# Layer 1's weight and rotation splits moved to GpSimd, in a two-layer attention trunk on one core

## The chip, the cores and the metric

The kernel runs on one core of one Trainium2 chip. The metric is device time in microseconds (us), the median of several executions. The engines are called as the profile calls them: PE (TensorE, the matmuls), PEld (its weight loads), DVE (VectorE), ACT (ScalarE), POOL (GpSimd) and SP (SyncE, which here issues every DMA). All arithmetic is float32. A product of two float32 operands is made from three matmuls: each operand is split into a rounded high part and the remaining low part, and high by high, high by low and low by high are summed.

## The reference, cut to what matters

Two decoder layers work on 1024 tokens of width 1024. Layer 0 mixes with a dilated sliding-window attention in three groups, layer 1 with a differential attention; each is followed by a gate, an output projection and a norm. The change is in layer 1, whose mixer is, shortened:

```
proj = h @ w_in
q = rope(proj[..., :1024]);  k = rope(proj[..., 1024:2048])
v = proj[..., 2048:3072];    gate = proj[..., 3072:]
for each head h of 8 and each block of 128 queries:
    s = q k^T / 8            # two score maps c = 0, 1, causal
    p = softmax(s)
    a = p[0] - lam * p[1]
    o = a @ v
y = (rmsnorm(o) * (1 - lambda_init) * silu(gate)) @ w_out
```

## The kernel before, in words

**Two kinds of order.** PE's instructions run in the order in which the program writes them (manual schedule for PE). The order on DVE, ACT, POOL and SP is set by a scheduler that simulates the program when it is built; each engine then runs its own list in order, and waits where an operand isn't ready.

**Units.** Layer 1's query and key projections are made in eight units, one a head, by `qk_unit` (L220), called with `on_pool=True` from `filler1` (L1022). A unit has two weight halves. Each half is loaded to `raw`, cast by ACT to `wh` (L184, the high part) and subtracted to `wl` (L122 through `split`, the low part). The tags `wh` and `wl` have three buffers, so a half can be split as soon as the half three places earlier has been used up; layer 1's value weights (`values1`, L811) take their turn in the same buffers.

A unit then makes four projections of 24 matmuls of 512 columns: two chunks of 512 tokens, each for both halves, into two PSUM banks (tag `pj`, L274, `pqk` in the trace). ACT copies each bank to an SBUF tile `x` (L243); POOL, which reads no PSUM here, rotates: four products and two sums, L247 to L252, into the tiles `r[0]` and `r[1]`. `x` has two buffers and L252 is the last reader of both, so the next chunk's copies wait for L252, and the matmuls that need the bank again wait for the copy. After the second chunk ACT casts each `r` to `rh` (L256), a subtraction overwrites `r` with its low part (L122 through `low`), and SP stores both to HBM (`qk_d`, L259), from where `heads_in` loads them as `qh`, `ql`, `ka` (L266, L268) when a head is due.

**Interleaving.** `Filler` feeds the units between the steps of the attention. First it runs 2.4 units alone (`LEAD1`), here called the lead; then each head's scores (L921, into two banks of tag `s`), exponentials (L931), transposes (L954), products with the values (L974) and norms alternate with the remaining units, value blocks and gates. DVE empties a score bank with the mask and the row minimum (L924); the matmuls of the score after next wait for that. Other DVE work in line with it: the minima (L927, L930), the combination of the two maps (L940, L941, L943), the low parts `pl` of the transposed weights, and the low parts of `wl` and `r`.

**Who subtracts, before.** `split` without an engine takes `alt()` (L125), which gives DVE and POOL in turn; in layer 1's units this puts the first half on POOL and the second on DVE. Both `r` subtractions of a layer 1 unit are on DVE (L257).

## Time and profile before

| | |
|---|---|
| median of 3 runs | 2029.63 us (2026.72 to 2030.63) |
| the profiled execution's own time | 2031.38 us |
| its span, first to last instruction | 2029.5 us |
| mean granted PE clock | 0.981 |
| layer 1's lead | about 1439 to 1495 us of the span |
| layer 1's interleaved part | about 1495 to 1960 us |

The profiled execution is one run of its own: 1.75 us above the median, with 1.9 us of its time outside the span. A timeline row gives the start, the duration, the engine, the line, the operation and its tiles, and in brackets the idle time of the engine just before it and what ended it. A row of the windows view gives busy time and instruction count of PE, PEld, DVE, ACT and POOL in a stretch, the granted PE clock, the share of busy DMA engines and GB/s.

### The profile page before, as it was taken

The page shows a single profiled execution, that of the slowest core. Times are in us where ns is not written, and L with a number is a line of the kernel's source. Part 1 is how long each engine was busy: PE and PEld are TensorE (multiplying, and loading weights), DVE is VectorE, ACT ScalarE, POOL GpSimd, SP SyncE. Part 2 cuts the span into 40 slices and gives each one's busy share as a digit, 9 for nine tenths or more (in the row PEclk, how much of TensorE's full clock was granted, in tenths as well). Part 3 has the DMA queues.
Part 4 walks back from the last instruction along what each step waited for, and adds up shares of the span by engine and source line. Part 5 has one row for each costly group of instructions (what it writes and reads, how often), then busy time and mean ns, then how long its engine had stood idle before and what let it go on. Part 6 is the DMA issues. An engine that isn't in the chain of part 4 may idle for free.

```text
span 2029.5 us, 28888 instructions
## 1 busy us (share of the span) xinstructions
PE 1905.9 (94%) x10008; PEld 1594.5 (79%) x10008; DVE 1143.0 (56%) x2771; ACT 888.0 (44%) x2057; POOL 618.0 (30%) x386
## 2 busy tenths in 40 slices
PE   6999999999999998989898978899999999999898
PEld 4788888888878787878787867788878788887776
DVE  3312122146676768676768674571057877878626
ACT  3312122125555555555555565352244445545632
POOL 2000000043353535353535340040471533524111
PEclk8999999999999999999999989999999999999999
DMA  5424244377696969697878889553356555555753
GB/s 208 146 88 140 87 156 152 113 221 229 191 300 195 291 202 293 195 282 218 267 234 240 256 284 294 162 176 107 129 174 193 175 176 164 169 196 182 274 160 125
DMA packets 218018, 397.90 MB, mean 196 GB/s; under 512 B 40976, under 2 KB 123408, under 8 KB 217872
## 3 DMA queue, kind: packets, MB, share of 16 engines
q1 hardware_dynamic: 217872, 396.04, 61.3%
q8 instruction: 80, 1.31, 0.3%
q14 instruction: 66, 0.54, 0.1%
HBM read 254.87 MB, written 132.71 MB: 191 GB/s over the span
## 4 chain that ended last, share of the span: by engine, by line
PE 62%; DMA 13%; DVE 12%; ACT 4%; POOL 4%; issue 3%; SPq 1%; POOLq 0%; DVEq 0%; ACTq 0%
PE pqk L274 22%; PE pv L213 16%; PE pg L274 8%; PE po L386 4%; PE sc L921 2%; PE pe L439 2%; PE up L646 2%; PE sc L596 2%; DMA wb<-wt_d 2%; PE ob L974 2%; DMA st_d<-st 2%; PE tp L619 2%; DVE u L669 1%; POOL r L252 1%; DVE pm L924 1%
## 5 line engine op out<-in xcount | busy, mean ns | idle before, releaser
L274 PE MATMUL pqk<-XL,wh 128*128 128x512 f32 x1024 | 421.1, 411 | 0.0
L274 PE MATMUL pqk<-XH,wh 128*128 128x512 f32 x1024 | 409.3, 400 | 1.7 <-DVE t L251 1.7
L274 PE MATMUL pqk<-XH,wl 128*128 128x512 f32 x1024 | 410.5, 401 | 0.0
L606 ACT ACTIVATE pm<-pm,st 128x128 f32<-128x128 f32 (+1 forms) x384 | 170.2, 444 | 159.7 <-DVE st L603 158.1
L122 POOL TENSOR_TENSOR wl<-raw,wh 128x1024 fp32r<-128x1024 f32 x35 | 84.0, 2400 | 500.6 <-ACT wh L184 500.6
L274 PEld LDWEIGHTS pqk<-XH,wh 128*128 128x128 f32 x1024 | 194.3, 190 | 30.6 <-DVE t L251 2.4
L274 PEld LDWEIGHTS pqk<-XL,wh 128*128 128x128 f32 x1024 | 194.4, 190 | 27.5
L274 PEld LDWEIGHTS pqk<-XH,wl 128*128 128x128 f32 x1024 | 194.8, 190 | 27.0
L250 POOL TENSOR_TENSOR r<-t 128x512 f32<-128x512 f32 x64 | 98.2, 1535 | 266.7 <-DVE t L249 265.7
L122 DVE TENSOR_TENSOR wl<-raw,wh 128x1024 fp32r<-128x1024 f32 x61 | 82.0, 1345 | 149.1 <-ACT wh L184 148.6
L213 PE MATMUL pv<-vwh,XH 128*128 128x512 f32 x384 | 155.8, 406 | 7.0 <-ACT XH L158 4.0
L184 ACT CAST wh<-raw 128x1024 fp32r<-128x1024 f32 x96 | 100.5, 1047 | 140.3 <-PE pqk L274 61.8
L213 PE MATMUL pv<-vwl,XH 128*128 128x512 f32 x384 | 154.9, 403 | 2.8 <-POOL vwl L122 2.8
L213 PE MATMUL pv<-vwh,XL 128*128 128x512 f32 x384 | 154.8, 403 | 0.9 <-DVE XL L122 0.3
L122 DVE TENSOR_TENSOR vs<-pv,vs 128x512 fp32r<-128x512 f32 x64 | 44.2, 691 | 197.3 <-ACT vs L513 191.3
L931 ACT ACTIVATE pm<-pm,mx 128x256 f32<-128x256 f32 (+7 forms) x128 | 99.4, 776 | 120.3 <-DVE mx L930 61.8
L122 DVE TENSOR_TENSOR pp<-tp,pp 128x512 fp32r<-128x512 f32 (+2 forms) x192 | 104.0, 542 | 73.6 <-ACT pp L623 72.0
L619 PE MATMUL tp<-ident,pm 128*128 128x128 f32 x560 | 95.7, 279 | 39.2 <-DVE pp L122 38.2
L603 DVE CUSTOM_DVE_ANT_0 pm<-sc,masks 128x128 f32<-128x128 f32 (+1 forms) x384 | 118.8, 344 | 20.8 <-PE sc L596 19.4
L619 PEld LDWEIGHTS tp<-ident,pm 128*128 128x128 f32 x560 | 72.6, 143 | 73.5 <-issue 34.2
L924 DVE CUSTOM_DVE_ANT_0 pm<-sc,md 128x512 f32<-128x512 f32 (+3 forms) x192 | 102.5, 551 | 32.9 <-PE sc L921 30.1
L513 ACT CAST vs<-pv 128x512 fp32r<-128x512 f32 x48 | 28.2, 587 | 189.9 <-PE pv L213 188.7
(514 smaller groups left out, 4483.6 us busy)
## 6 DMA issues: line engine op xcount, KB each, us to landing
qk_d<-rh SPq DMA_DIRECT2D x64, 512.0 KB
qk_d<-r SPq DMA_DIRECT2D x64, 512.0 KB
qh<-qk_d SPq DMA_DIRECT2D x128, 256.0 KB
ql<-qk_d SPq DMA_DIRECT2D x128, 256.0 KB
ka<-qk_d SPq DMA_DIRECT2D x64, 512.0 KB
v_d<-vs SPq DMA_DIRECT2D x48, 512.0 KB
raw<-in_dil_qk_dram SPq DMA_DIRECT2D x48, 512.0 KB
vt<-v_d SPq DMA_DIRECT2D x48, 512.0 KB
```

The costliest lines, as they stand in the source:

```text
L122: eng.tensor_tensor(o, full, hi.bitcast(F32), ALU.subtract)
L184: nc.scalar.copy(wh, raw)
L213: nc.tensor.matmul(o, lhsT=l, rhs=r_, start=first and k == 0, stop=last and k == 3 * KT - 1, skip_group_check=True)
L250: nc.gpsimd.tensor_sub(put(r[0]), nat(t1), nat(t2))
L274: nc.tensor.matmul(o, lhsT=l[:, kt, :], rhs=r_[:, kt, tok], start=kt == 0 and k == 0, stop=kt == KT - 1 and k == 2)
L386: nc.tensor.matmul(banks[c], lhsT=l[:, kt, ts(n)], rhs=r_[:, ts(c, 512)], start=first and k == 0, stop=last and k == 2,)
L439: nc.tensor.matmul(bank, lhsT=l[:, kt, ts(n)], rhs=r_[:, ts(c, 512)], start=kt == 0 and k == 0, stop=kt == EARLY - 1 and k == 2)
L603: nc.vector.tensor_tensor_reduce(pm[:, cols], sc[:, cols], m[:, m.shape[1] - w_ :], 1.0, 3.0e38, ALU.add, ALU.min, st[:, 0, j : j + 1])
L606: nc.scalar.activation(pm[:, cols], pm[:, cols], AF.Exp, bias=st[:, 0, j : j + 1], scale=-1.0, accum_out=st[:, 1, j : j + 1])
L619: nc.tensor.transpose(out=tp[:, ts(n)], in_=self.pb.pop((b, kb)), identity=ident)
L924: nc.vector.tensor_tensor_reduce(pm[:, k0:k1], sc[:, :w_], m_, 1.0, 3.0e38, ALU.add, ALU.min, mx[:, j : j + 1])
L931: nc.scalar.activation(pm[:, :wq], pm[:, :wq], AF.Exp, bias=mx[:, 0:1], scale=-1.0, accum_out=den)
```

## The change

In layer 1's units both weight halves' subtractions, and both `r` subtractions, are given to POOL. Layer 0's calls (`on_pool=False`) still take `alt()`.

```
-            split(wh, wl, load(w[half], [P, KT, P]))
+            split(wh, wl, load(w[half], [P, KT, P]), nc.gpsimd if on_pool else None)
...
-            low(nc.vector if on_pool else alt(), r[e].bitcast(F32R), r[e], rh)
+            low(nc.gpsimd if on_pool else alt(), r[e].bitcast(F32R), r[e], rh)
```

Each unit made two calls of `alt()` in `split`, an even number, so every later user of `alt()` keeps its engine. Eight `wl` and sixteen `r` subtractions of 128x1024 move from DVE to POOL. PE's list is unchanged; the scheduler's lists for DVE, ACT, POOL and SP are the same up to the end of layer 1's gates, and differ in places after that.

POOL, in the lead, from the first unit's second chunk (`x_13168`, `x_13169`) to the second unit's first (`x_13258` is its first product). `wl_13339` is the third unit's first half. Before:

```order
L247 TENSOR_TENSOR t_13172<-x_13168,cos_2235 128x512
L248 TENSOR_TENSOR x_13168<-x_13168,sin_2236 128x512
L122 TENSOR_TENSOR wl_13339<-raw_13340,wh_13338 128x1024
L249 TENSOR_TENSOR t_13173<-x_13169,sin_2236 128x512
L250 TENSOR_TENSOR r_13054<-t_13172,t_13173 128x512
L251 TENSOR_TENSOR x_13169<-x_13169,cos_2235 128x512
L252 TENSOR_TENSOR r_13055<-x_13169,x_13168 128x512
L247 TENSOR_TENSOR t_13258<-x_13254,cos_2235 128x512
```

Now, in the same place (`wl_13197` is the second unit's second half):

```order
L122 TENSOR_TENSOR wl_13197<-raw_13198,wh_13196 128x1024
L247 TENSOR_TENSOR t_13172<-x_13168,cos_2235 128x512
L248 TENSOR_TENSOR x_13168<-x_13168,sin_2236 128x512
L122 TENSOR_TENSOR wl_13339<-raw_13340,wh_13338 128x1024
L249 TENSOR_TENSOR t_13173<-x_13169,sin_2236 128x512
L250 TENSOR_TENSOR r_13054<-t_13172,t_13173 128x512
L251 TENSOR_TENSOR x_13169<-x_13169,cos_2235 128x512
L122 TENSOR_TENSOR r_13054<-r_13054,rh_13180 128x1024
L252 TENSOR_TENSOR r_13055<-x_13169,x_13168 128x512
L122 TENSOR_TENSOR r_13055<-r_13055,rh_13185 128x1024
L247 TENSOR_TENSOR t_13258<-x_13254,cos_2235 128x512
```

A `wl` stands ahead of the chunk, one `r` ahead of its L252, and the other `r` ahead of the next unit's first product.

ACT, the end of the second unit (`x_13316` and `x_13317` are the copies of its second chunk) to the first copy of the third (`x_13467`), as a difference. `wh_13344` is the third unit's second half, `wh_13652` the first value weights after it, `pm0` and `pm1` the first exponentials of head 0:

```order
 L184 CAST wh_13344<-raw_13346 128x1024
+L184 CAST wh_13652<-raw_13654 128x1024
 L243 COPY x_13316<-pqk_13266 128x512
-L184 CAST wh_13652<-raw_13654 128x1024
 L243 COPY x_13317<-pqk_13291 128x512
 L256 CAST rh_13328<-r_13202 128x1024
+L931 ACTIVATE pm0_13414,den_13393<-pm0_13414,mx0_13415 128x128
+L931 ACTIVATE pm1_13423,mx1_13424<-pm1_13423,mx1_13424 128x128
 L256 CAST rh_13333<-r_13203 128x1024
 L243 COPY x_13467<-pqk_13352 128x512
```

The cast of the value weights, whose buffer comes free when the second unit's last projection ends, now stands ahead of the copy of that unit's third projection; and two exponentials stand ahead of the second `rh`.

DVE, around the fourth unit's `r` subtractions, at the start of head 2 (`pm_14660` and `pm_14688` are score tiles), as a difference:

```order
 L122 TENSOR_TENSOR pl<-tp,ph 128x512
-L122 TENSOR_TENSOR r<-r,rh 128x1024
 L924 ISA pm_14660,mx_14661<-sc,md 128x128
 L924 ISA mx_14661 128x1
-L122 TENSOR_TENSOR r<-r,rh 128x1024
 L940 RECIPROCAL mx_14661<-mx_14661 128x1
+L941 SCALAR_TENSOR_TENSOR mx_14661<-mx_14661,neg_lam,den 128x1
+L943 SCALAR_TENSOR_TENSOR pm_14641<-pm_14660,mx_14661,pm_14641 128x128
 L924 ISA pm_14688,mx_14689<-sc,md 128x256
```

The two `r` rows go, and L941 and L943 of the map before move up into the room.

## The prediction

> **What bounds the kernel now.** I read the page first, then the windows of layer 1, PE's waits there, and the timelines of the engines around them. The page's first part:

> ```profile
> PE 1905.9 (94%) x10008; PEld 1594.5 (79%) x10008; DVE 1143.0 (56%) x2771; ACT 888.0 (44%) x2057; POOL 618.0 (30%) x386
> ```

> PE is the bound, and DVE or POOL matter only where PE waits for them. The windows view (PE, PEld, DVE, ACT, POOL busy; PE clock; DMA share; GB/s) splits layer 1's attention: two stretches of one unit each in the lead, then the interleaved part.

> ```profile
> 1439.20:1461.70 22.50, 22.50 (x99) 18.23 (x98) 1.23 (x1) 5.74 (x8) 13.28 (x9) 1.00 0.46 155
> 1461.70:1484.20 22.50, 22.50 (x98) 18.02 (x97) 3.68 (x3) 6.34 (x9) 19.07 (x13) 1.00 0.67 206
> 1497.00:1960.00 463.00, 434.70 (x2670) 381.31 (x2670) 342.26 (x940) 239.72 (x468) 164.75 (x112) 0.99 0.56 180
> ```

> In the lead a unit takes PE 22.5 us without a gap, so a projection takes 5.6 us; POOL is busy for 19.07 of the second 22.5 us and DVE for 3.68. In the interleaved part it is the other way about: DVE is 74% busy, POOL 36%. PE's waits from 1440 to 1960 us (total, times, longest):

> ```profile
> PE sc L921 <- DVE mx L924: 18.3, 18, 2.5
> PE sc L921 <- issue: 3.8, 1, 3.8
> PE sc L921 <- DMA ka<-qk_d: 1.1, 1, 1.1
> ```

> What there is to win is mainly the 18.3 us in which a score's matmuls wait until DVE has emptied their bank. PE doesn't wait for POOL anywhere, but in the lead it is a near thing. ACT there:

> ```profile
> 1471.03 1.05 ACT L256 CAST rh<-r 128x1024 fp32r<-128x1024 f32 x1 [2.44 <-POOL r L252]
> 1471.99 0.58 ACT L243 COPY x<-pqk 128x512 f32<-128x512 f32 x1
> 1483.85 1.05 ACT L184 CAST wh<-raw 128x1024 fp32r<-128x1024 f32 x1 [1.46 <-PE pqk L274]
> ```

> and PE, at the projection that reuses the bank which that copy empties:

> ```profile
> 1472.62 0.50 PE L274 MATMUL pqk<-XH,wh 128*128 128x512 f32 x1
> ```

> L252 ends at 1471.0, the cast and the copy follow, the copy ends at 1472.57 and the projection starts at 1472.62. The slack is nil: whatever delays this L252 delays PE.

> **The change part by part.** The groups view of 1440 to 1960 us gives the moved work (count, busy us, mean ns):

> ```profile
> L122 DVE TENSOR_TENSOR wl<-raw,wh 128x1024 fp32r<-128x1024 f32 x16 | 21.6, 1351 | 39.3 <-ACT wh L184 39.1
> L122 DVE TENSOR_TENSOR r<-r,rh 128x1024 fp32r<-128x1024 f32 x16 | 21.2, 1330 | 19.6 <-ACT rh L256 19.6
> L122 POOL TENSOR_TENSOR wl<-raw,wh 128x1024 fp32r<-128x1024 f32 x9 | 21.6, 2401 | 71.3 <-ACT wh L184 71.3
> ```

> DVE loses 8 x 1.35 + 16 x 1.33 = 32.1 us, POOL gains 24 x 2.40 = 57.6 us. Seven of the 24 belong to the lead (three `wl`, four `r`), seventeen to the interleaved part, which has 12 `r` and 5 `wl`.

> *The lead.* A unit would cost POOL 19.07 + 3 x 2.40 = 26.3 us against PE's 22.5, so POOL can't keep up there. The rows that I step through are these of POOL:

> ```profile
> 1462.48 2.40 POOL L122 TENSOR_TENSOR wl<-raw,wh 128x1024 fp32r<-128x1024 f32 x1 [1.82 <-ACT wh L184]
> 1464.84 1.30 POOL L249 TENSOR_TENSOR t<-x,sin 128x512 f32<-128x512 f32 x1
> 1467.46 1.29 POOL L251 TENSOR_TENSOR x<-x,cos 128x512 f32<-128x512 f32 x1
> 1468.84 2.17 POOL L252 TENSOR_TENSOR r<-x 128x512 f32<-128x512 f32 x1
> ```

> The extra `wl` ahead of the first unit's second chunk fits into the idle 1.82 us and the rest before 1462.48, where POOL must wait for ACT's cast anyway, so L251 still ends at 1468.75. Then `r` (2.40) and L252 (1.30, since no DVE work crosses it any more) end at 1472.5 instead of 1471.0. Cast and copy end at 1474.1, and PE waits from 1472.7 to about 1474.1: 1.4 us. The second `r` starts only after its cast, at 1473.6, and ends at 1476.0; the second unit's first chunk, with a `wl` in it, then ends at 1476.0 + 5 x 1.3 + 2.4 + 1.3 = 1486.2. Meanwhile PE finishes that unit at 1485.4 and wants its bank back. On ACT the cast of the value weights now stands ahead of that copy, and its buffer comes free only at PE's end: cast 1.05 and copy 0.58, 1487.0, so PE waits 1.7 us more. After that the attention is mixed in, a unit takes PE longer than POOL, and POOL catches up. Together **+3.1 us**. The bounds: 0 if the scheduler's order leaves the copies earlier than I read it, and 6.5 if each wait also brings 1.7 us of lower clock. Two windows, the first after PE's longest wait for DVE, the second after a shorter one, and that shorter wait:

> ```profile
> 1525.50:1528.90 3.40, 3.40 (x19) 3.40 (x18) 2.49 (x6) 2.15 (x4) 0.00 (x0) 0.50 0.48 189
> 1870.70:1874.10 3.40, 3.40 (x21) 2.88 (x21) 3.38 (x10) 3.33 (x6) 0.00 (x0) 1.00 0.53 151
> ```

> ```profile
> 1867.51 0.51 PE L921 MATMUL sc<-ka,qh 128*128 128x512 f32 x1 [2.08 <-DVE mx L924]
> ```

> Half clock for 3.40 us followed a wait of 2.53 us (its row is below), full clock one of 2.08 us; I take no loss for waits of 1.4 and 1.7. [...]

> *The relief.* Where DVE's own `r` stood ahead of a bank that PE waited for, the wait should go (timeline rows of DVE and PE, in order of time):

> ```profile
> 1493.36 1.23 DVE L122 TENSOR_TENSOR r<-r,rh 128x1024 fp32r<-128x1024 f32 x1 [2.27 <-ACT rh L256]
> 1494.85 0.39 PE L921 MATMUL sc<-ka,qh 128*128 128x256 f32 x1 [0.83 <-DVE mx L924]
> 1608.78 1.22 DVE L122 TENSOR_TENSOR r<-r,rh 128x1024 fp32r<-128x1024 f32 x1
> 1610.46 0.45 PE L921 MATMUL sc<-ka,qh 128*128 128x384 f32 x1 [0.81 <-DVE mx L924]
> 1613.24 0.44 PE L921 MATMUL sc<-ka,qh 128*128 128x384 f32 x1 [1.24 <-DVE mx L924]
> 1667.06 0.33 PE L921 MATMUL sc<-ka,qh 128*128 128x128 f32 x1 [1.13 <-DMA ka<-qk_d]
> 1728.31 0.44 PE L921 MATMUL sc<-ka,qh 128*128 128x384 f32 x1 [1.25 <-DVE mx L924]
> 1733.17 0.50 PE L921 MATMUL sc<-ka,qh 128*128 128x512 f32 x1 [0.31 <-DVE mx L924]
> 1738.69 0.38 PE L921 MATMUL sc<-ka,qh 128*128 128x256 f32 x1 [1.53 <-DVE mx L924]
> ```

> I count 0.83, 0.81, 0.31 and 1.13 whole (the load of `ka` was issued behind a store that waited for DVE after two `r`), and half of 1.24, 1.25 and 1.53, where other DVE work was late as well: **-5.1 us**, between -3.1 and -7.1.

> *The price.* POOL's work holds up DVE. In the timelines, POOL first, then DVE and PE:

> ```profile
> 1515.73 2.40 POOL L122 TENSOR_TENSOR wl<-raw,wh 128x1024 fp32r<-128x1024 f32 x1 [3.91 <-ACT wh L184]
> ```

> ```profile
> 1516.39 1.77 DVE L927 TENSOR_TENSOR mx<-mx 128x1 f32<-128x1 f32 x1
> 1519.51 1.27 DVE L941 SCALAR_TENSOR_TENSOR mx<-mx,neg_lam,den 128x1 f32<-128x1 f32 x1
> 1520.81 1.99 DVE L943 SCALAR_TENSOR_TENSOR pm<-pm,mx,pm 128x768 f32<-128x768 f32 x1
> ```

> ```profile
> 1523.46 0.50 PE L921 MATMUL sc<-ka,qh 128*128 128x512 f32 x1 [2.53 <-DVE mx L924]
> 1563.21 0.38 PE L921 MATMUL sc<-ka,qh 128*128 128x256 f32 x1 [0.72 <-DVE mx L924]
> 1849.39 0.39 PE L921 MATMUL sc<-ka,qh 128*128 128x256 f32 x1 [1.38 <-DVE mx L924]
> ```

> ```profile
> L927 DVE TENSOR_TENSOR mx<-mx x64: 140/155/2252, 1507.2 to 1932.6; 128x1 f32<-128x1 f32 x64
> ```

> A subtraction of one element a partition, 155 ns as a rule, took 1.77 us and ended when POOL's 2.40 us piece did. Seven pieces of 2.40 us already run on POOL in the interleaved part (the group's nine less two in the lead), and three of PE's waits (2.53, 0.72, 1.38) come within a few us after one: 0.66 us a piece at most, and nothing at the least, since in the first of them later POOL work shares the blame. I take 0.3, nearer the two plain cases spread over seven: 17 x 0.3 = **+5.1 us**, between 0 and 11.2.

> [...]

> *At no cost.* The `r` stores to HBM start up to 2.7 us later in the lead; the first score there starts 3 us later too. Later units are stored most of a head before they are loaded. POOL's `r` work delays L1004 (the norm's power) by at most one piece, in front of a gate that is due later. ACT's work is the same in amount.

> The sum is 3.1 - 5.1 + 5.1 = +3.1 us: 2034.5 against the profiled execution's own 2031.38. That execution is 1.75 us above the median, 2029.63; against the median it is **2032.7 us**.

> **The rivals.** A difference under 0.2% (4 us) can hardly be told from none in this kernel.

> *POOL's backlog lasts (slower).* The waits of the lead are read whole or worse: the copy of the third unit's first projection is also late, because two exponentials and a second `r` stand ahead of it (about 2 us), and one wait brings half clock (1.7 us): 3.1 + 2 + 1.7 = 6.8. It decides if PE loses over 5 us before 1500 us. For it: POOL's 26.3 against 22.5 us. Against: 2.4 units only.

> *The lock eats the relief (slower).* Every added piece holds DVE for half its length: 17 x 1.2 = 20.4 us against 17 x 1.34 = 22.8 us taken off in the interleaved part, so DVE wins nothing and the pieces come at moments that the scheduler didn't plan. With 0.66 us a piece and the relief at 3.1: 3.1 - 3.1 + 11.2 = +11.2, or 2040.8. It decides if DVE's mean for L927, L941 and L943 rises. The two together are what "slower" stands for: 2038 in the middle.

> *DVE's relief carries (faster).* The lead's waits are hidden and the added pieces meet DVE in L924 and `pl`: 0 - 7.1 + 1 = -6, 2023.6. For it: 74% busy on DVE, 36% on POOL. Against: the nil slack at 1472.6.

> **How the numbers follow.** The forecast, a change too small to tell: 0.45. The two slower rivals together 0.40, since two separate mechanisms lead there and the sum already leans that way; faster 0.15. The range goes from -4.6 (most of the faster rival) to +10.4 (just short of the lock's full price): 2025 to 2040.

> **What would show it.** Right: POOL's idle time in the lead gone; PE idle for 1 to 2 us near 1473 and near 1486, each ended by ACT's copy; no `r` ahead of the first score; POOL about 58 us and DVE about 12 to 20 us changed in busy time over layer 1; PE's wait for L924 near 18 us still. Wrong: PE without a gap before 1495 us, or its wait for L924 below 10 or above 28 us.

## The result and the profile after

The changed kernel takes 2041.65 us, the median of its five undisturbed runs (2040.24 to 2045.93; a sixth, at 2623.72 us and a granted clock of 0.656 against 0.976 to 0.980 in the five, is left out). The kernel before, run beside it, takes 2032.03 us over six runs. The ratio, worked out over the runs, is 1.0055, with a 95% interval from 1.0035 to 1.0075 (the two medians, 9.6 us apart, give 1.0047): slower by about 0.5%. The forecast was +3.1 us and 2032.7 us, with 2040 as the upper end; both were too low. The profiled execution took 2044.94 us, with a span of 2043.1.

The page's first part, of the kernel after:

```profile
PE 1912.1 (94%) x10008; PEld 1599.8 (78%) x10008; DVE 1136.3 (56%) x2747; ACT 886.1 (43%) x2057; POOL 666.5 (33%) x410
```

POOL has 48.5 us more and DVE only 6.7 us less, though 24 pieces of 1.3 us left DVE and came to POOL at 2.40 us. The windows of the lead and of the interleaved part (PE, PEld, DVE, ACT, POOL busy; PE clock; DMA share; GB/s):

```profile
1461.70:1484.20 22.50, 21.23 (x92) 16.91 (x91) 0.00 (x0) 6.13 (x8) 20.11 (x13) 1.00 0.36 134
...
1497.00:1973.00 476.00, 444.51 (x2708) 388.83 (x2707) 347.93 (x931) 241.78 (x477) 214.83 (x136) 0.99 0.55 181
```

In this stretch of the lead DVE now does nothing at all (0.00 us) while POOL is busy for 20.11 of 22.5 us, and PE has lost its unbroken 22.50. PE's waits from 1440 to 1975 us (total, times, longest):

```profile
PE sc L921 <- DVE mx L924: 18.8, 17, 2.5
PE tp L954 <- DVE pl L122: 4.1, 4, 2.2
PE pqk L274 <- ACT x L243: 2.7, 2, 1.4
...
PE sc L921 <- issue: 2.2, 1, 2.2
...
PE sc L921 <- DMA ka<-qk_d: 1.2, 1, 1.2
```

The wait for L924 is where it was (18.3 before), and the two waits for ACT's copies `x` are new. They are the forecast's two, as PE's rows and ACT's rows ahead of them show (the cast of `rh` ahead of the first copy, the cast of the value weights ahead of the second):

```profile
1480.18 0.50 PE L274 MATMUL pqk<-XH,wh 128*128 128x512 f32 x1 [1.27 <-ACT x L243]
...
1493.07 0.50 PE L274 MATMUL pqk<-XH,wh 128*128 128x512 f32 x1 [1.43 <-ACT x L243]
```

```profile
1478.60 1.05 ACT L256 CAST rh<-r 128x1024 fp32r<-128x1024 f32 x1 [3.81 <-POOL r L252]
1479.55 1.06 ACT L243 COPY x<-pqk 128x512 f32<-128x512 f32 x2
...
1491.49 1.04 ACT L184 CAST wh<-raw 128x1024 fp32r<-128x1024 f32 x1 [4.55 <-PE pqk L274]
1492.44 1.07 ACT L243 COPY x<-pqk 128x512 f32<-128x512 f32 x2
```

**Where the time went.** PE's list is the same in every kernel below, so the start of the same matmul can be compared between two traces. The two profiled executions were already 6.2 us apart at the start of layer 1, in code that is unchanged and runs in the same order on PE, DVE, ACT and POOL; that is chance (the last section says what goes with it) and is taken off. What a kernel adds to the trace of before from there on, worked out from the starts of PE's matmuls at 1400, 1493, 1596 and 1795 us of before and at the end:

| kernel | lead, to 1493 | first heads, to 1596 | to 1795 | to the end | sum |
|---|---|---|---|---|---|
| whole change, first profile | +3.1 | +5.4 | +3.4 | -4.6 | +7.3 |
| whole change, second profile | +3.1 | +7.6 | +5.1 | -4.6 | +11.1 |
| `lead_only` | +3.1 | +3.5 | -0.3 | +0.9 | +7.2 |
| `later_only` | 0.0 | -0.4 | +3.6 | -1.6 | +1.6 |
| `lead_r_dve` | +0.1 | +2.9 | +6.7 | -2.7 | +6.9 |
| `short_rope` | +0.8 | -3.7 | -2.9 | -4.0 | -9.7 |

Single profiles differ by some 3 us, so the sums are a map and the medians decide. The lead's +3.1 is the forecast to a tenth, and then comes as much again that the forecast didn't have.

DVE's operations were held more often. The groups of four operations of DVE that have two inputs in SBUF (count, busy us, mean ns), before and after, over the same 1497 to 1985 us:

```profile
L943 DVE SCALAR_TENSOR_TENSOR pm<-pm,mx,pm 128x128 f32<-128x128 f32 (+3 forms) x64 | 62.7, 980 | 1.2
L941 DVE SCALAR_TENSOR_TENSOR mx<-mx,neg_lam,den 128x1 f32<-128x1 f32 x64 | 22.7, 355 | 1.3
L927 DVE TENSOR_TENSOR mx<-mx 128x1 f32<-128x1 f32 x64 | 22.0, 344 | 0.7
...
L1005 DVE TENSOR_TENSOR nr<-nr,nd 128x4 f32<-128x4 f32 x16 | 4.7, 296 | 12.8 <-POOL nr L1004 12.8
```

```profile
L943 DVE SCALAR_TENSOR_TENSOR pm<-pm,mx,pm 128x128 f32<-128x128 f32 (+3 forms) x64 | 71.9, 1124 | 1.3
...
L927 DVE TENSOR_TENSOR mx<-mx 128x1 f32<-128x1 f32 x64 | 25.0, 391 | 0.8
L941 DVE SCALAR_TENSOR_TENSOR mx<-mx,neg_lam,den 128x1 f32<-128x1 f32 x64 | 24.1, 376 | 1.4
...
L1005 DVE TENSOR_TENSOR nr<-nr,nd 128x4 f32<-128x4 f32 x16 | 9.3, 583 | 12.0 <-POOL nr L1004 12.0
```

Their sum goes from 112.1 to 130.3 us for the same work. "The four groups" below is this sum; it gauges how long POOL holds DVE. Some expectations use a wider gauge, "DVE's excess": what all of DVE's operations of the interleaved part took beyond the time of the same operation undisturbed, 54.5 us before and 74 to 75 in the two profiles after.

### The profile page after: what moved, and what is told of

Same layout as the page of the kernel before. It is cut to its first block, busy times and chain, and to the rows that moved or that the text cites. A ratio compares the mean times of both kernels' runs of the same rounds, so it can differ in the third digit from the quotient of the medians.

```text
span 2043.1 us, 28875 instructions
## 1 busy us (share of the span) xinstructions
PE 1912.1 (94%) x10008; PEld 1599.8 (78%) x10008; DVE 1136.3 (56%) x2747; ACT 886.1 (43%) x2057; POOL 666.5 (33%) x410
## 5 line engine op out<-in xcount | busy, mean ns | idle before, releaser
L274 PE MATMUL pqk<-XL,wh 128*128 128x512 f32 x1024 | 423.5, 414 | 0.0
L274 PE MATMUL pqk<-XH,wh 128*128 128x512 f32 x1024 | 411.0, 401 | 4.3 <-ACT x L243 2.7
L274 PE MATMUL pqk<-XH,wl 128*128 128x512 f32 x1024 | 412.8, 403 | 0.0
L122 POOL TENSOR_TENSOR wl<-raw,wh 128x1024 fp32r<-128x1024 f32 x43 | 104.0, 2418 | 495.8 <-ACT wh L184 495.7
L274 PEld LDWEIGHTS pqk<-XH,wh 128*128 128x128 f32 x1024 | 195.3, 191 | 34.8 <-ACT x L243 3.6
L274 PEld LDWEIGHTS pqk<-XH,wl 128*128 128x128 f32 x1024 | 196.3, 192 | 27.2
L274 PEld LDWEIGHTS pqk<-XL,wh 128*128 128x128 f32 x1024 | 195.7, 191 | 27.6
L122 DVE TENSOR_TENSOR wl<-raw,wh 128x1024 fp32r<-128x1024 f32 x53 | 70.4, 1329 | 168.0 <-ACT wh L184 167.9
L184 ACT CAST wh<-raw 128x1024 fp32r<-128x1024 f32 x96 | 100.5, 1047 | 144.6 <-PE pqk L274 71.1
L122 DVE TENSOR_TENSOR vs<-pv,vs 128x512 fp32r<-128x512 f32 x64 | 44.1, 689 | 196.6 <-ACT vs L513 191.8
L122 DVE TENSOR_TENSOR pp<-tp,pp 128x512 fp32r<-128x512 f32 (+2 forms) x192 | 103.8, 541 | 75.3 <-ACT pp L623 73.7
L924 DVE CUSTOM_DVE_ANT_0 pm<-sc,md 128x512 f32<-128x512 f32 (+2 forms) x192 | 102.9, 550 | 39.1 <-PE sc L921 36.4
```

Of the source, the lines that this page charges most:

```text
L122: eng.tensor_tensor(o, full, hi.bitcast(F32), ALU.subtract)
L184: nc.scalar.copy(wh, raw)
L274: nc.tensor.matmul(o, lhsT=l[:, kt, :], rhs=r_[:, kt, tok], start=kt == 0 and k == 0, stop=kt == KT - 1 and k == 2)
L924: nc.vector.tensor_tensor_reduce(pm[:, k0:k1], sc[:, :w_], m_, 1.0, 3.0e38, ALU.add, ALU.min, mx[:, j : j + 1])
```

## The experiments

Three theories stood against one another. *Lead*: the loss is paid in units 24 to 26 and the first heads. *Lock*, the forecast's word for DVE's operations held while a piece of POOL runs: the pieces hold DVE and eat what it was relieved of. *Order*: the scheduler's order alone. All times are medians with the kernel before run beside them (2032.6 to 2034.5 us); the ratios are worked out over the runs. Code is cut to the lines that differ, from the kernel after in `r_only`, `wl_only`, `lead_r_dve` and `x_dve`, from the kernel before in the others.

| kernel | us | ratio to before | 95% interval | four groups, us |
|---|---|---|---|---|
| `r_only` | 2040.21 | 1.0032 | 1.0016 to 1.0048 | 127.3 |
| `wl_only` | 2035.16 | 0.9998 | 0.9984 to 1.0013 | 115.1 |
| `later_only` | 2034.82 | 1.0000 | 0.9986 to 1.0015 | 126.6 |
| `no_sub` | 2027.06 | 0.9960 | 0.9943 to 0.9977 | 102.3 |
| `lead_only` | 2039.24 | 1.0036 | 1.0023 to 1.0049 | 113.4 |
| `again` | 2042.42 | 1.0046 | 1.0030 to 1.0062 | 131.5 |
| `extra_sub` | 2065.88 | 1.0167 | 1.0149 to 1.0185 | 134.0 |
| `extra_set` | 2033.18 | 1.0004 | 0.9992 to 1.0016 | 107.3 |
| `extra_set5` | 2039.41 | 1.0032 | 1.0018 to 1.0047 | 110.4 |
| `extra_short` | 2050.12 | 1.0086 | 1.0060 to 1.0111 | 126.8 |
| `quarters` | 2040.54 | 1.0034 | 1.0020 to 1.0048 | 115.2 |
| `wl_dve` | 2034.75 | 1.0007 | 0.9993 to 1.0021 | 107.2 |
| `lead_r_dve` | 2036.16 | 1.0017 | 1.0002 to 1.0032 | 132.1 |
| `x_dve` | 2047.34 | 1.0072 | 1.0053 to 1.0092 | 132.4 |
| `short_rope` | 2024.19 | 0.9958 | 0.9943 to 0.9973 | 97.3 |

### Which part costs

**`r_only`**: the change's second line alone.

```
-            split(wh, wl, load(w[half], [P, KT, P]), nc.gpsimd if on_pool else None)
+            split(wh, wl, load(w[half], [P, KT, P]))
```

> Only the sixteen r subtractions of layer 1 go to POOL; the weight halves stay in turn on POOL and DVE. The lock theory (each POOL piece of 2.4 us in the interleaved part holds up DVE, and what DVE is spared is eaten by that): 12 of the 17 pieces of the interleaved part are here, about 0.5 us each, so +6 us, and +1.4 to +3 us in the lead from the r that stands ahead of L252: +7 to +9 us against before, DVE's L927, L941 and L943 together some 14 us longer. The backlog theory (POOL can't keep up in the lead, the rest is even): +3 to +5 us, all of it before the first score. The theory that it is only the scheduler's new order: anything within 5 us of before, unrelated to the count of pieces.

**`wl_only`**: its first line alone.

```
-            low(nc.gpsimd if on_pool else alt(), r[e].bitcast(F32R), r[e], rh)
+            low(nc.vector if on_pool else alt(), r[e].bitcast(F32R), r[e], rh)
```

> Only the second weight halves go to POOL; the r subtractions stay on DVE. Lock: 5 pieces of the interleaved part, +2 to +3 us against before, no wait in the lead. Backlog: under +2 us, POOL's extra 2.4 us a unit fits into the lead. Order: anything within 5 us of before.

**`later_only`**: both lines, `nc.gpsimd` only if `unit >= 27`; as before in units 24 to 26.

> The change for units 3 to 7 alone, so that nothing of it lies in the lead: 15 pieces of 2.4 us, all in the interleaved part. Lock: 15 x 0.5 = +7 to +8 us against before, with no wait of PE for ACT's copies before the first score. Backlog: no change against before, within 2 us. Order: within 5 us of before, either way.

**`no_sub`**: no subtraction in layer 1's units at all; the third matmul of a projection reads `wh` again, and `r` is stored as it is in place of its low part.

```
-        low(eng or alt(), wl, raw, wh)
+        eng == 0 or low(eng or alt(), wl, raw, wh)
...
-            split(wh, wl, load(w[half], [P, KT, P]))
-            tiles.append((wh, wl))
+            split(wh, wl, load(w[half], [P, KT, P]), 0 if on_pool else None)
+            tiles.append((wh, wh if on_pool else wl))
...
-            low(nc.vector if on_pool else alt(), r[e].bitcast(F32R), r[e], rh)
+            on_pool or low(alt(), r[e].bitcast(F32R), r[e], rh)
```

> Layer 1's 32 subtractions of both kinds are left out on every engine (the third matmul takes the high part again, and the full r is stored as its low part), so that neither DVE nor POOL does them. Lock: DVE's relief without a price, and POOL's own eight pieces gone too: -7 to -12 us against before. Backlog: -5 us, the relief that was forecast. Order: no sign can be told, within 5 us of before.

`r_only` has most of the loss, `wl_only` and `later_only` have none that shows (their intervals are 3 us wide to either side). For `later_only` the lock theory had asked for +7 to +8 us; measured is 1.0000, although the four groups rose to 126.6. So from unit 27 on the holds and the relief come to nothing in the sum, and the loss that shows lies in units 24 to 26. All 32 subtractions together are worth 0.4% (`no_sub`), 7.4 us; its interval doesn't tell the lock theory's -7 to -12 from the -5 of the others.

**`lead_only`**: the reverse of `later_only`, `nc.gpsimd` only if `24 <= unit < 27`. **`again`**: the whole change unaltered.

> The splits and the halves r of units 24 to 26 alone go to POOL; from unit 27 on all is as before. The lead theory (what the change costs is paid in the lead and in the first heads, where DVE has nothing else to do and POOL is in the way of ACT's copies of x and of the heads' own loads): +6 to +10 us against before, all of it ahead of 1580 us of the trace, with the two waits of PE for ACT's x (1.28 and 1.43 us in the changed kernel) there again. The lock theory (a piece on POOL holds DVE's operations for 1.2 us, 17 times, in the interleaved part): +2 to +4 us, the two waits alone.

> The whole change once more, as a yardstick for the parts and for a second profile of it. Every theory: +8 to +12 us against before; the waits of PE in layer 1 between 30 and 35 us in its profile, 32.7 us the first time. If it comes out under +5 us, the first result was high by chance, and the prediction's +3 would be near.

The lead theory is borne out: +0.36%, against +0.46 and +0.55% for the whole. The two parts add up within their intervals; the 3 us by which the medians of the whole (+9.5 and +9.6 us) lie above that of `lead_only` (+6.4) are placed by no run. PE's waits of `lead_only` from 1440 to 1600 us:

```profile
PE sc L921 <- DVE mx L924: 5.8, 4, 2.5
PE pqk L274 <- ACT x L243: 2.7, 2, 1.4
PE sc L921 <- DMA ka<-qk_d: 0.8, 1, 0.8
PE tp L954 <- DVE pl L122: 0.5, 1, 0.5
```

The waits for `x` are 2.7 us of the +7.2 in its trace. Comparing matmul by matmul with before gives the next +3.5: PE is 3.1 us behind at 1485 us, 1.9 at 1501, 2.9 at 1506.5, 4.4 at 1510.5, 5.5 at 1548 (the 0.55 us for `pl` is in it) and 6.5 at 1553. Two waits of before, 0.83 and 1.76 us, became one of 2.40, at 1506.78, no loss by itself, but behind it the granted clock was 0.50 for 3.40 us. Held operations had a part in that wait: at 1498.60 and 1499.43 DVE's L941 and L943 took 0.80 and 1.48 us, against 0.22 and 0.48 in before, under POOL's late `r` and the rotation behind it. The windows around the wait:

```profile
1503.60:1507.00 3.40, 1.00 (x5) 0.60 (x4) 3.40 (x5) 0.18 (x1) 3.32 (x3) 1.00 0.01 2
1507.00:1510.40 3.40, 3.40 (x10) 2.73 (x10) 2.86 (x11) 2.30 (x4) 0.45 (x1) 0.50 0.00 0
```

PE is idle for 2.40 of the first 3.40 us, and the second stretch runs at 0.50; over it the matmuls fall 1.5 us further behind. Of the last us, 0.81 is a wait for the second head's keys, at 1553.43. That head's own `r` went out by 1500 us; what is late is the third unit's. Its stores stood ahead of all loads of the second head on SP, and now two of them stand between these loads. SP before, then in `lead_only`:

```profile
1528.01 0.52 SPq L259 DMA_DIRECT2D qk_d<-r  x1
1531.27 1.13 SPq L266 DMA_DIRECT2D qh<-qk_d  x2
...
1538.95 0.58 SPq L268 DMA_DIRECT2D ka<-qk_d  x1
```

```profile
1533.83 0.49 SPq L266 DMA_DIRECT2D qh<-qk_d  x1
1534.42 0.54 SPq L259 DMA_DIRECT2D qk_d<-rh  x1
...
1536.58 0.56 SPq L259 DMA_DIRECT2D qk_d<-r  x1
...
1543.64 0.51 SPq L268 DMA_DIRECT2D ka<-qk_d  x1
```

The last load of the keys goes out 9.8 us after the head's first load, 7.7 before.

**`lead_r_dve`**: the whole change, with the six `r` of the lead back on DVE.

```
-            low(nc.gpsimd if on_pool else alt(), r[e].bitcast(F32R), r[e], rh)
+            low(nc.gpsimd if unit >= 27 else nc.vector if on_pool else alt(), r[e].bitcast(F32R), r[e], rh)
```

> The whole change, except that the halves r of units 24 to 26 stay on DVE, which does nothing in the lead; the weights' splits of all units and the r from unit 27 on are on POOL. If the six r pieces of the lead are what costs (ACT's x waits behind the cast of rh, and the first heads' keys come late): no wait for x, no wait for ka in the second head, and 0 to +3 us against before, so that 6 us and more of the whole change's loss are gone. If the loss sits in all pieces alike (lock theory by count, 6 of 17): two thirds of it stay, +6 to +8 us.

+0.17%: by the two ratios about two thirds of the loss goes with six of the 24 pieces. The upper end of its expectation, +3 us, is just passed (2036.16 against 2032.63). PE's waits from 1440 to 1600 us have one row left, no `x`, no `ka`, and the third unit's stores stand ahead of the second head's loads again:

```profile
PE sc L921 <- DVE mx L924: 8.2, 7, 2.5
```

**`x_dve`**: the whole change, with the lead's copies `x` taken from ACT.

```
-                    nc.scalar.copy(x[i], pp[i])
+                    (nc.vector.tensor_copy if unit < 27 else nc.scalar.copy)(x[i], pp[i])
```

> The whole change, with the copies x of units 24 to 26 made by DVE in place of ACT, so that they don't stand behind the casts of rh on ACT. If the two waits of PE for x (1.28 and 1.43 us) come from ACT's order, they shrink to under 0.5 us each, and what follows from them does too: 2 to 5 us faster than the whole change. If x waits for POOL to let its tile go, the waits stay above 1 us and the time is that of the whole change.

A miss. The first wait went: the copy now starts as soon as POOL's L252 lets its tile go (DVE's first row below). The second grew from 1.43 to 2.90 us, since on DVE the copy stands behind a split of weights that waits for its own cast:

```profile
1474.77 1.29 DVE L243 COPY x<-pqk 128x512 f32<-128x512 f32 x2 [9.86 <-POOL r L252]
1487.88 1.23 DVE L122 TENSOR_TENSOR wl<-raw,wh 128x1024 fp32r<-128x1024 f32 x1 [11.81 <-ACT wh L184]
1489.02 1.28 DVE L243 COPY x<-pqk 128x512 f32<-128x512 f32 x2
```

So ACT's order makes the first wait, and moved to DVE the second copy is late again, behind other work in line. Whether the whole is slower than the change isn't shown, since the intervals overlap; a wait of 4.68 us near 1535 us in its trace stays unexplained.

The order theory wasn't tested by itself. DVE's list of layer 1's attention differs from that of before in every kernel of the table, so an effect of some us from a new order can lie in any of the differences. Against it as the main cause: the two waits for `x` are the same, 1.3 and 1.4 us, in all three traces with the lead's whole pieces on POOL and the copies on ACT, and `lead_r_dve` and `later_only` have none.

### What a piece on POOL costs

**`extra_sub`**, **`extra_set`**, **`extra_set5`**, **`extra_short`**: before, with extra work on POOL behind each half of the weights of units 27 to 31, written to the tile `raw`, which nobody reads any more. Nothing is taken from DVE.

```
-            split(wh, wl, load(w[half], [P, KT, P]))
-            tiles.append((wh, wl))
+            split(wh, wl, raw := load(w[half], [P, KT, P]))
+            [low(nc.gpsimd, raw, raw, wh) for _ in range(2 * (unit >= 27))]; tiles.append((wh, wl))
```

In `extra_set` the call is `nc.gpsimd.memset(raw, 0.0)`, in `extra_set5` five of it, in `extra_short` eight subtractions of two of the eight tiles each.

> Before, with two subtractions 128x1024 more on POOL behind each half of the weights of units 27 to 31 (20 in all; they write to a tile that is no longer read). Nothing is taken from DVE, so this is the price alone. The lock theory: each holds DVE's operations for about 1.2 us, some 20 to 24 us of holds in the sum, and the kernel is 7 to 12 us slower. The lead theory: the holds fall mostly where PE has work in hand, 0 to +4 us.

> The same as extra_sub, but each of the 20 pieces is a memset of 128x1024 on POOL, which reads nothing. If what a piece costs is POOL's time in its queue, this costs as extra_sub does in proportion to the pieces' length. If it is DVE held while POOL reads and writes the memory, DVE's operations show the same excess as before (54.5 us) or hardly more, and the time is within 2 us of before.

> As extra_set, but five memsets 128x1024 on POOL behind each half of the weights of units 27 to 31 (50 in all, 0.97 us each in the trace of extra_set, 48.5 us), so that POOL is busy as long as with the 20 subtractions of extra_sub (49.8 us). The lock theory (what costs is DVE held while POOL subtracts): within 3 us of before, DVE's excess as before. The queue theory (POOL's other work comes late): near extra_sub, +25 us or more.

> As extra_sub, but each of its 20 subtractions is cut into four of 128x256 (80 in all, about 0.75 us each, some 60 us of POOL's time). If a piece of DVE that comes into a subtraction of POOL is held to that subtraction's end, the longest hold falls from 2.4 to 0.8 us and the price from +33 us to +10 to +18 us. If DVE is only slowed for as long as POOL works, the price is as high as before or higher, +33 to +40 us.

Twenty subtractions cost 33 us, 1.65 us each, far beyond any expectation. Fifty memsets, which keep POOL as long (47.7 us against 49.8), cost 5.0 to 6.5 us: that is POOL's queue, and PE's waits for the keys show it (7.6 us in that trace). The rest goes with DVE's holds, but not as waiting alone. From 1440 us on PE's waits come to 45.4 us in `extra_sub`, against 29.8 before, and the slots at half clock to 53.2 us, against 15.9. At half their length, an estimate, the clock took 18.7 us more and the waits 15.6: over half of the price is the clock that follows the waits. POOL's and DVE's rows of `extra_sub`, and the wait of PE that followed:

```profile
1743.71 2.40 POOL L122 TENSOR_TENSOR raw<-raw,wh 128x1024 f32<-128x1024 f32 x1 [3.75 <-DVE wl L122]
```

```profile
1743.59 0.16 DVE L940 RECIPROCAL mx<-mx 128x1 f32<-128x1 f32 x1
1743.79 2.34 DVE L941 SCALAR_TENSOR_TENSOR mx<-mx,neg_lam,den 128x1 f32<-128x1 f32 x1
1746.16 2.25 DVE L943 SCALAR_TENSOR_TENSOR pm<-pm,mx,pm 128x1024 f32<-128x1024 f32 x1
```

```profile
1748.93 0.44 PE L954 MATMUL tp<-ident,pm 128*128 128x128 f32 x2 [2.59 <-DVE pl L122]
```

L941 took 0.22 us when alone (its median in before). It started 0.08 us into the piece and ended with it. With memsets, in `extra_set5`, POOL and DVE run past each other; L941 starts 0.09 us into the memset, L943 inside it too, and both take what they take alone (in before 0.22 us, the median of L941, and 1.28, the shortest L943 of 128x1024):

```profile
1723.95 0.95 POOL L226 MEMSET raw<- 128x1024 f32 x1 [3.73 <-DVE wl L122]
```

```profile
1724.04 0.22 DVE L941 SCALAR_TENSOR_TENSOR mx<-mx,neg_lam,den 128x1 f32<-128x1 f32 x1
1724.30 1.28 DVE L943 SCALAR_TENSOR_TENSOR pm<-pm,mx,pm 128x1024 f32<-128x1024 f32 x1
```

Counted over the interleaved part of `extra_sub`: of the operations of L927, L941, L943 and L1005 that start inside one of POOL's tensor operations, with room to end in it, 53 of 58 are held (three of the others started inside L1004, POOL's power of 128x4); of L924 and `pl`, which read PSUM, none of 136. In the traces of before and after, from 1497 to 1985 us, the same count gives 36 of 39 and 49 of 51 held of the four, none of 96 and 147 of L924 and `pl`. L930, with one input in SBUF, took 156 ns at the longest in either. In `extra_set5` twelve of the four kinds start inside a memset with room to end in it, and none is held. An L1001 (one input, 128x4; its median in before is 0.17 us) took 4.02 us there under six memsets without a gap. Under POOL's tensor operations L1001 took up to 1.28 us in before; what sets it apart from L930 no run shows. The expectation for the memsets was right in the four groups (110.4, before 112.1). DVE's excess, 77 us, says otherwise only because 21 us of it are this one stall, to whose end seven operations in line are recorded.

`extra_short` has the same subtractions in 128x256, 0.85 us apiece. It costs 15.7 us in place of 33, as expected if a hold lasts to the end of a piece, so that shorter pieces hold less. The four groups fall only from 134.0 to 126.8 us, though; PE's waits from 1440 us on fall from 45.4 to 37.4 us, and the slots at half clock from 53.2 to 26.6.

**`quarters`**: the whole change, with its subtractions on POOL cut into four the same way.

> The whole change, with each of its 32 subtractions on POOL cut into four of 128x256. The lock theory, with holds to the end of a piece: DVE's excess falls from 74 to 75 us to about 62, and the kernel is 5 to 9 us faster than the whole change, +1 to +5 us against before; the lead's waits for x stay, or grow by some tenths since the pieces together are longer. The lead theory alone: as the whole change, +9 to +12 us.

DVE's excess falls to 59 us and the four groups to 115.2, nearly as before, which was expected; but the time falls only to +0.34%, 2 to 4 us below the whole change where 5 to 9 were expected, and the intervals of the two overlap. What may have taken the gain back stands in its trace: the waits for `x` grew to 3.2 us, and two waits for keys come to 7.4.

**`wl_dve`**: `nc.vector` in both lines, all 32 subtractions of the layer's units on DVE.

> The opposite of the change: all 32 subtractions of layer 1 on DVE. The lock theory: 7 pieces less on POOL in the interleaved part, at 1.65 us each, against 7 pieces more in DVE's own queue: within 4 us of before. If the queue of DVE is what counts, +4 to +8 us; if POOL's pieces cost as extra_sub says and DVE's pieces hide, -4 to -10 us, and it is the version to take.

No difference, within 4 us: what DVE's eight further pieces cost and what POOL's fewer holds give (four groups 107.2 us, before 112.1) come out even.

**`short_rope`**: before, with POOL's pieces shorter: six rotations of 128x512 as two of 128x256 each, and the splits that `alt()` gives to POOL in four.

```
+            cut = lambda f, *ts_: [f(*(t[:, k : k + 512 // h_] for t in ts_)) for k in range(0, 512, 512 // h_)]
+            h_ = 2 if on_pool else 1
...
-            eng.tensor_mul(t4, x[1], cos[:, tok])
+            cut(eng.tensor_mul, t4, x[1], cos[:, tok])
```

> Before, with r on DVE as it was, and every piece of POOL in layer 1's attention units cut shorter: the six rotations of 128x512 into two of 128x256 each, the splits of weights that fall to POOL into four. The lock theory, with holds to the end of a piece: DVE's excess falls from 54.5 us to 35 to 42, and the kernel is 2 to 6 us faster than before, the version to take. If holds off the path are all that is left in before, or POOL's longer sum makes the lead wait: within 2 us of before.

It beats both kernels: 2024.19 against 2032.63 us, ratio 0.9958 (0.9943 to 0.9973), a little more than expected. DVE's excess falls to 37 us, the four groups to 97.3, and PE's wait for the emptied score banks, 18.3 us before, is halved. That fits the holds; what the scheduler's new order gave wasn't separated from it (line numbers here are higher by one or two):

```profile
PE sc L923 <- DVE mx L926: 9.4, 11, 2.2
...
PE pqk L276 <- ACT x L244: 0.8, 1, 0.8
```

## Why the prediction was wrong

- *The lead, +3.1: right.* Forecast were 1.4 us near 1473 and 1.7 near 1486, each ended by ACT's copy; measured 1.27 and 1.43 us, ending at 1474 and 1487 when the 6.2 us of chance are taken off. PE fell 3.1 us behind before the first score, in both profiles of the change and in `lead_only`.
- *"At no cost": this is the step that failed.* It took the lead's late work as made up by the first heads and looked at each store only from the side of its own reader. The third unit's late stores delay another unit's loads on SP: the second head waits for its keys, 0.8 us in `lead_only` and 1.2 and 1.6 in the two profiles of the whole change. And two of the first heads' waits meet in one of 2.40 us, behind which the granted clock was 0.50. In `lead_only` that is +3.5 us beside the +3.1. The term of the lead with its consequences should have been 6 to 7 us (6.4 by the medians, 7.2 in the trace).
- *The lower clock, bounded with 1.7 us a wait (half of 3.40 us, an estimate) and taken as nothing: half right.* Neither wait for `x` brought it in `lead_only`; a wait 20 us later did, and cost 1.5 us.
- *Relief -5.1 and price +5.1: the sum was right, the sizes were not shown so.* From unit 27 on they come to nothing in the sum (`later_only`, 1.0000). But a piece without relief costs 1.65 us (`extra_sub`), not 0.3; some 0.3 of that is POOL's queue alone (`extra_set5`, 5.0 to 6.5 us for the time of twenty pieces), and over half is lower clock (by the estimate above), which the price of 0.3 didn't hold at all. What the relief by itself is worth, and whether a piece of the change costs as much as one of `extra_sub`, which stands right behind another, was not separated.
- *The rivals.* "The lock eats the relief" is what happened from unit 27 on: its sign came (the means of L927, L941 and L943 rose by 14, 6 and 15%), and holds grew by 18 us in the four groups where I had priced 20.4. But it is a wash, not the +8 that stood on top. "POOL's backlog lasts" had about the right amount, +6.8, in part by luck: its half clock came, but its mark was over 5 us lost before 1500, and 3.1 were; the rest came after, from other waits than the copy that it named. "DVE's relief carries" had the added pieces meet DVE in L924 and `pl`: neither was held in after (none of 147), but the four groups were (49 of 51), and the time came out longer.
- *The busy times: wrong.* Named were about 58 us more on POOL and 12 to 20 less on DVE; over the whole span they are 48.5 and 6.7. DVE's held operations ate most of what it was spared, and POOL's rotations got shorter (L252 from 27.1 to 22.3 us, L247 from 27.0 to 23.9, from 1440 to 1985 us), which fits fewer pieces of DVE in their way: the L252 at 1468.84 of before, beside DVE's `r` of 1468.62 to 1469.85, took 2.17 us, that at 1477.27 of after, with DVE idle, 1.29.
- *What it was measured against.* Before came out at 2032.03, 2.4 us above the median that the forecast started from. Of the 9 us by which the forecast missed, 2.4 are that.

## What to carry to other kernels

Moving work to an idle engine is to be judged stage by stage: here the pieces were a wash where DVE was 74% busy, and a loss in the stage where DVE did nothing and POOL was already busy for 85% of the time. What starts late in a lead is followed through its store to whatever stands behind that store in SP's list, before it is called free. And since L927, L941, L943 and L1005, DVE's operations with two inputs in SBUF, waited to the end of POOL's piece in 53 of 58 cases in `extra_sub` and in 49 of 51 in after, POOL's pieces beside them are kept short here: the kernel with the shorter pieces was 0.4% faster, while moving them gained nothing.

## What the hardware showed that I had not expected

```profile
1863.40:1866.80 3.40, 2.03 (x11) 1.40 (x10) 2.21 (x6) 1.39 (x3) 0.42 (x1) 1.00 0.47 151
1866.80:1870.20 3.40, 2.69 (x17) 2.43 (x18) 2.82 (x15) 1.58 (x3) 1.02 (x1) 1.00 0.01 4
1522.10:1525.50 3.40, 1.83 (x10) 1.39 (x11) 3.40 (x10) 1.05 (x1) 1.83 (x1) 1.00 0.39 154
```

The first two share the wait of 2.08 us that kept full clock in the prediction: 1.37 and 0.71 us idle. The third is idle for 1.57 us, the larger part of the wait of 2.53, and half clock followed. So of two waits of much the same length, 2.08 and 2.40 us (the second in `lead_only`, whole in the 3.40 us before 1507.00), the one was followed by 1.00 and the other by 0.50.

**The same code varies, in part by this.** Up to 1400 us of before the program and its order on PE, DVE, ACT and POOL are the same in all these kernels, yet the end of that part lay between 3.0 us earlier and 6.2 us later than in the first profile of before. Behind its first 50 us, half clock cost it 23.9 us in the trace of before and 30.7 in that of after (half the length of its slots, 47.8 and 61.4 us, an estimate), and PE's waits came to 65.5 and 67.7 us. A difference of a few us is read from medians, or from one stage of two traces set to the same start.
